# Long branch B: probabilities transposed in blocks of 32 by VectorE and through DRAM; value products by halves, three units behind

## The chip, the cores and the metric

The kernel runs on one NeuronCore of a Trainium2 chip. Its five engines have instruction streams of their own: TensorE (PE; PEld is its weight load), VectorE (DVE), ScalarE (ACT), GpSimd (POOL) and SyncE (SP). SP, ACT and POOL also issue DMA transfers, each from its own queue in order. The metric is the device time of one execution in microseconds; smaller is better.

## The reference

One layer of an encoder with two token mixers, on a prompt of 1024 tokens and a sample of 512, model width 1024, everything in float32. Branch A is grouped-query attention with rotary positions, branch B neighbourhood attention on a grid 64 tokens wide: a query sees a clamped window of 8 rows by 16 columns, with a learned bias. Cut to what matters here:

```python
def _token_mixer(xn, ...):
    z = xn @ w_in                       # q, k, v of both branches, two gates
    o_a = _gqa_attention(qa, ka, va)
    o_b = _neighbourhood_attention(qb, kb, vb, rpb)
    merged = sigmoid(ga) * (o_a @ w_proj_a) + sigmoid(gb) * (o_b @ w_proj_b)
    return merged @ w_out

    # _neighbourhood_attention, for each block of 128 queries
    s = einsum('bqhd,bkhd->bhqk', qi, kb) * scale + bias
    s = where(mask, s, NEG_INF)
    p = softmax(s, axis=-1)
    return einsum('bhqk,bkhd->bqhd', p, vb)
```

Two residual blocks (this mixer, then an MLP with squared ReLU) and a final norm follow.

## The kernel before

Products of full accuracy are made of three PE products in a reduced format: each operand is split into a high part (a ScalarE copy that rounds, `hi`) and the rest (`lo`, source minus `hi`, mostly on VectorE). The helper `mm3` (L195 to L197) adds hi x hi, hi x lo and lo x hi into one PSUM bank. `load_cols` (L223) brings weights by SP into one of three staging buffers (`raw_tile`, 3 buffers shared by all such loads of the long run) and splits them (`split`, L184 on ScalarE, L190 on VectorE).

`run` handles the sample first (512 tokens, `NB` = 1) and then the prompt (1024 tokens, `NB` = 2, "long"). In each, branch A comes first, then branch B, then both projections. The change is in branch B of the long run, the phase `phB`.

Branch B works in 32 units: 8 heads times 4 strips `j` of 16 query columns, in the order 1, 2, 0, 3. A unit of the long run has two halves (`hf`) of 128 queries (8 rows by 16 columns), and for each half 384 keys (12 rows by 32 columns).

- `s_unit`: two score products a half (L971) into the PSUM tile `sb` ("sbs" in the profile, two buffers of pool `pbig`), VectorE adds bias and mask, negates and reduces (L974), ScalarE takes the exponential and its sum (L979), VectorE the reciprocal (L981), POOL scales (L982) to the probabilities `pb` ("pbs"). POOL also adds bias and mask (`bms`, L957). `prep` brings a head's bias (`rects`) and value strips (`vss`, sixteen DMAs, L878).
- `t_unit`: PE transposes 128x128 blocks of `pb` by products with the identity (L994), three a half, into PSUM `ptb`; ScalarE rounds them into `bh` (L999), VectorE subtracts for the rest (L1000).
- `v_unit`: value strips times transposed probabilities (L1013) into `ob`: key blocks 1 and 2 for both halves (512 columns: hi and lo times 256 queries), blocks 0 and 3 for one half each (256 columns). `finish_o` adds the parts and sends heads 0 to 5 to DRAM (`obd`); heads 6 and 7 stay.

The loop calls `s_unit` for unit i, `t_unit` for unit i - `LS`, `v_unit` for unit i - `LS` - `LV` (both 1 in the long run). Between them, `fill.pull` takes PE work from generators: the branch B gate (`gate`, "gpss") and, for the last eight units, branch A's output projection (`proj_a`, "ppas": eight columns of weights `raw_pas`, activations `rawos` split into `oXs`, gate values `zas`). Every eight units `qkproj` makes queries and keys of the next two heads ("pqbs", "pkbs").

This order of calls is not the order on the engines. The tile scheduler orders each engine's stream when the program is built, and it moves loads and products ahead where their buffers are free in its plan. On the chip every stream, SP's DMA queue too, runs in that fixed order, and an instruction that waits holds all behind it.

## Time and profile before

| what | value |
|---|---|
| median of 3 runs | 2145.7 us (2145.51 to 2145.97) |
| profiled execution, first to last instruction (its span) | 2144.2 us |
| branch B of the long run in it | 777 to 1067 us |
| PE, granted clock | busy in 99% of the span, 0.999 of full speed |
| HBM | 264.85 MB read, 87.88 MB written |

The profiled execution has only its span on record; the runs lie about 1.5 us above it, from what stands before the first and after the last instruction. In rows of instruction groups the order is: line, engine, operation, out<-in, shapes, count, then busy us and mean ns, then idle time of the engine before them and who ended it. Rows of the timeline are: start, duration, engine, line, operation. A PE product's shown duration includes its way through the array; how long it holds PE is read from the distance of the starts.

### The profile page before, as it was taken

Reading aid. Unit: us, or ns where it says so; the run is one execution under the profiler, and the core shown is the slowest. Engines: PE = TensorE matmul, PEld = TensorE weight load, DVE = VectorE, ACT = ScalarE, POOL = GpSimd, SP = SyncE. Lnnn points to the kernel's source line nnn. Section 1 sums busy time; section 2 is a strip of 40 time slices with the busy share of each in tenths; the row PEclk is TensorE's granted clock in tenths of the full one; section 3 lists DMA queues with packets and bytes.
Section 4 is the critical chain, followed back from the end, with each engine's and each line's share of the span. In section 5 each row is a group of like instructions: output and inputs, shape, how many; then the busy total and the mean of one; then the engine's idle time right before and its main releaser. Section 6 shows DMA issues by size and latency. Waiting matters only on the chain.

```text
span 2144.2 us, 32083 instructions
## 1 busy us (share of the span) xinstructions
PE 2116.2 (99%) x10967; PEld 1847.3 (86%) x10967; DVE 1462.7 (68%) x2793; ACT 1146.2 (53%) x2511; POOL 356.1 (17%) x446
## 2 busy tenths in 40 slices
PE   9999999999999999999999999999999999999998
PEld 8888778888897888887888899999999988888886
DVE  6665786767657755656882877777777777659563
ACT  6664653767566644555530566566655643434342
POOL 2232310323232223333200200003000000000000
PEclk9999999999999999999999999999999999999999
DMA  6437557520122133444472665578545799688561
GB/s 190 133 98 212 152 162 251 186 71 25 57 79 68 42 95 108 131 118 112 140 240 103 213 194 184 171 248 205 165 142 157 256 353 343 212 279 281 165 206 59
DMA packets 321259, 354.08 MB, mean 165 GB/s; under 512 B 31551, under 2 KB 255431, under 8 KB 321095
## 3 DMA queue, kind: packets, MB, share of 16 engines
q1 hardware_dynamic: 277927, 279.65, 41.9%
q10 hardware_dynamic: 36016, 52.19, 7.0%
q0 software_dynamic: 7152, 20.19, 3.5%
q8 instruction: 87, 1.43, 0.3%
q14 instruction: 77, 0.63, 0.1%
HBM read 264.85 MB, written 87.88 MB: 165 GB/s over the span
## 4 chain that ended last, share of the span: by engine, by line
PE 67%; DVE 1%; issue 1%; DMA 0%; ACT 0%; POOL 0%; SPq 0%; POOLq 0%; ACTq 0%; DVEq 0%
PE dn L195 6%; PE dn L196 6%; PE dn L197 6%; PE ua L195 2%; PE ua L196 2%; PE ua L197 2%; PE ud L195 2%; PE ud L196 2%; PE ud L197 2%; PE uc L195 2%; PE uc L196 2%; PE uc L197 2%; PE gpss L195 2%; PE gpss L197 2%; PE gpss L196 2%; PE ops L197 1%
## 5 line engine op out<-in xcount | busy, mean ns | idle before, releaser
L197 PE MATMUL dn<-wd,al 128*128 128x512 f32 x624 | 242.8, 389 | 0.0
L196 PE MATMUL dn<-wd,ah 128*128 128x512 f32 x624 | 242.8, 389 | 0.0
L195 PE MATMUL dn<-wd,ah 128*128 128x512 f32 x624 | 242.7, 389 | 0.0
L1273 ACT ACTIVATE ah<-ar 128x512 fp32r<-128x512 f32 x168 | 104.4, 628 | 203.1 <-PE dn L196 177.1
L1274 DVE TENSOR_TENSOR al<-ar,ah 128x512 fp32r<-128x512 f32 x168 | 113.9, 685 | 71.6 <-ACT ah L1273 64.0
L197 PEld LDWEIGHTS dn<-wd,al 128*128 128x128 f32 x624 | 117.1, 188 | 24.4
L195 PEld LDWEIGHTS dn<-wd,ah 128*128 128x128 f32 x624 | 117.1, 188 | 24.3
L196 PEld LDWEIGHTS dn<-wd,ah 128*128 128x128 f32 x624 | 117.1, 188 | 24.2
L749 POOL TENSOR_SCALAR ps<-ps,rls 128x1024 f32<-128x1024 f32 (+1 forms) x96 | 96.8, 1010 | 225.7 <-DVE rls L748 200.4
L788 ACT ACTIVATE pths<-pTs 128x512 fp32r<-128x512 f32 x160 | 94.0, 597 | 74.0 <-PE pTs L783 71.9
L789 DVE TENSOR_TENSOR ptls<-pTs,pths 128x512 fp32r<-128x512 f32 x160 | 107.6, 686 | 37.7 <-ACT pths L788 36.9
L743 DVE TENSOR_REDUCE nms<-ss 128x1 f32<-128x1024 f32 (+1 forms) x96 | 99.8, 1040 | 25.6 <-PE ss L741 25.0
L195 PE MATMUL gpss<-xs_0h,w_gs 128*128 128x512 f32 x256 | 105.5, 412 | 0.5 <-DVE ot_Bs L440 0.4
L746 ACT ACTIVATE ps<-ss,nms 128x1024 f32<-128x1024 f32 (+1 forms) x96 | 93.2, 972 | 22.8 <-DVE nms L743 20.2
L783 PEld LDWEIGHTS pTs<-ident,ps 128*128 128x128 f32 x640 | 77.9, 140 | 28.5 <-POOL ps L749 4.3
L180 POOL TENSOR_TENSOR rs_f<-ms_f,mhalf 128x1 f32<-128x1 f32 x6 | 4.0, 667 | 590.7 <-DVE ms_f L176 590.7
L197 PE MATMUL gpss<-xs_0h,w_gs 128*128 128x512 f32 x256 | 101.1, 395 | 0.2 <-DVE w_gs L190 0.2
L196 PE MATMUL gpss<-xs_0l,w_gs 128*128 128x512 f32 x256 | 101.0, 394 | 0.0
L783 PE MATMUL pTs<-ident,ps 128*128 128x128 f32 x640 | 99.0, 274 | 1.3 <-DVE ptls L789 0.6
L1273 ACT ACTIVATE A<-S 128x512 fp32r<-128x512 f32 x128 | 75.9, 623 | 31.5 <-DVE S L1336 22.7
L957 POOL TENSOR_TENSOR bms<-rects,msks 128x384 f32<-128x384 f32 (+1 forms) x72 | 70.1, 977 | 129.1 <-DVE nmbs L974 107.6
L1392 ACT ACTIVATE c<-c 128x384 f32<-128x384 f32 x96 | 50.3, 524 | 69.4 <-DVE c L1391 69.3
(330 smaller groups left out, 6419.7 us busy)
## 6 DMA issues: line engine op xcount, KB each, us to landing
ar<-ud SPq DMA_DIRECT2D x120, 512.0 KB, 5.3
br<-in_w_mlp_down_dram SPq DMA_DIRECT2D x72, 512.0 KB, 5.2
rawu<-in_w_mlp_up_dram SPq DMA_DIRECT2D x64, 512.0 KB, 4.1
ud<-c ACTq DMA_DIRECT2D x128, 192.0 KB, 3.2
raw_gs<-in_w_in_dram SPq DMA_DIRECT2D x32, 512.0 KB, 4.0
zgs<-sgs ACTq DMA_DIRECT2D x48, 256.0 KB, 2.2
ud<-cs SPq DMA_DIRECT2D x64, 192.0 KB
raw_os<-in_w_out_dram SPq DMA_DIRECT2D x16, 512.0 KB, 3.9
```

Source lines behind the costliest of these rows:

```text
L195: nc.tensor.matmul(out, ah, bh, start=start, stop=False, **kw)
L196: nc.tensor.matmul(out, ah, bl, start=False, stop=False, **kw)
L197: nc.tensor.matmul(out, al, bh, start=False, stop=stop, **kw)
L743: nc.vector.tensor_reduce(nm_, s, axis=AX.X, op=ALU.max, negate=True)
L746: nc.scalar.activation(p, s, AF.Exp, bias=nm_, accum_out=l)
L749: nc.gpsimd.tensor_scalar(p, p, rl, 1.0, op0=ALU.mult, op1=ALU.mult)
L783: nc.tensor.transpose(pt[:, j * P : (j + 1) * P], PP[u, j][:, kc * P : (kc + 1) * P], ident)
L788: nc.scalar.activation(hi, pt, AF.Copy)
L789: nc.vector.tensor_tensor(lo, pt, hi.bitcast(F32), op=ALU.subtract)
L957: nc.gpsimd.tensor_tensor(bm.rearrange("p (r c) -> p r c", c=32), rects[h][:, ir : ir + kr_n, jr : jr + 32], msk[:, hf * 3 + ct, :].rearra ...
L1273: nc.scalar.activation(hi, src, AF.Copy)
L1274: nc.vector.tensor_tensor(lo, src, hi.bitcast(F32), op=ALU.subtract)
```

## The change

For the long run only (`moved`): the exponential writes its 384 columns into one tile `pb` for both halves, ordered by 32-column block. VectorE transposes the 128x768 tile in place in blocks of 32x32 (L1001 of the changed kernel). SP writes it to a DRAM tile (`tbs`, L1003), and one step later, in `fetch_t`, reads it back with four DMAs (L1012) so that the four 32-row groups of queries stand beside each other and keys lie on partitions. The four reads land in the lo part of `bh` (three buffers instead of two); `t_unit` is then one ScalarE copy of 768 columns for hi (L1022) and one POOL subtraction in place for lo (L1023). The PE transposes, their PSUM tiles, and the two copies and two VectorE subtractions are gone in the long run. `v_unit` makes six products of 256 columns, one for each half and key block (L1049), instead of four. `LS` is 2 for both runs, so value products come three units behind the scores. `pb` has two buffers of twice the size instead of four. `finish_o` takes `os` at the width it uses.

```diff
--- before.py
+++ after.py
@@ -443,12 +443,12 @@
                 nc.scalar.activation(t[:, :n], o[HD:P, :n], AF.Copy)
             if parts is not None:
                 hi, lo, ps = parts
-                b = pool.tile([P, 512], F32, tag="os", name=f"os_{nm}", bufs=2)[ps, :n]
+                b = pool.tile([P, n], F32, tag="os", name=f"os_{nm}", bufs=2)[ps, :n]
                 nc.vector.tensor_tensor(b, o[0:HD, :n], t[:, :n], op=ALU.add)
                 nc.scalar.activation(hi, b, AF.Copy)
                 nc.vector.tensor_tensor(lo, b, hi.bitcast(F32), op=ALU.subtract)
                 return
-            b = pool.tile([HD, 512], F32, tag="os", name=f"os_{nm}", bufs=2)
+            b = pool.tile([HD, n], F32, tag="os", name=f"os_{nm}", bufs=2)
             nc.vector.tensor_tensor(b[:, :n], o[0:HD, :n], t[:, :n], op=ALU.add)
             nc.scalar.dma_start(dst, b[:, :n])
 
@@ -861,6 +861,7 @@
             msk = ph.tile([P, halves * 3, nkey], BF16, tag="msk", name=f"msk{N}", bufs=1)
             nc.gpsimd.dma_start(msk, w["mask2"] if halves == 2 else w["mask1"])
             rects, strips, bms, PT = {}, {}, {}, {}
+            moved = NB == 2
 
             def raw_here(name):
                 if NB == 2:
@@ -948,6 +949,8 @@
                 jr = (16, 8, 8, 0)[j]
                 s = big(f"sb{N}_{h}_{j}")
                 ps = []
+                if moved:
+                    pm = ph.tile([P, 4, halves, nkc, 32], F32, tag="pb", name=f"pb{N}_{h}_{j}", bufs=2)
                 for hf in range(halves):
                     nm = f"{N}_{h}_{j}_{hf}"
                     r0 = 0 if hf == 0 else 4
@@ -974,18 +977,51 @@
                     nc.vector.tensor_tensor_reduce(
                         out=sb, in0=so, in1=bm, op0=ALU.add, op1=ALU.min, scale=-1.0, scalar=3e38, accum_out=nm_
                     )
-                    p = ph.tile([P, nkey], F32, tag="pb", name=f"pb{nm}", bufs=4)
                     l = sml.tile([P, 1], F32, tag="l", name=f"lb{nm}")
-                    nc.scalar.activation(p, sb, AF.Exp, bias=nm_, scale=-1.0, accum_out=l)
+                    if moved:
+                        p = pm[:, :, hf]
+                        nc.scalar.activation(
+                            p.rearrange("p b k i -> p k b i"),
+                            sb.rearrange("p (k b i) -> p k b i", b=4, i=32),
+                            AF.Exp,
+                            bias=nm_,
+                            scale=-1.0,
+                            accum_out=l,
+                        )
+                    else:
+                        p = ph.tile([P, nkey], F32, tag="pb", name=f"pb{nm}", bufs=4)
+                        nc.scalar.activation(p, sb, AF.Exp, bias=nm_, scale=-1.0, accum_out=l)
                     rl = sml.tile([P, 1], F32, tag="rl", name=f"rlb{nm}")
                     nc.vector.reciprocal(rl, l)
                     nc.gpsimd.tensor_scalar(p, p, rl, 1.0, op0=ALU.mult, op1=ALU.mult)
                     ps.append(p)
                 PT[u] = ps
+                if moved:
+                    blocks = pm.rearrange("p b f k i -> p (b f k) i")
+                    nc.vector.transpose(blocks, blocks)
+                    turned = dram.tile([P, 4, halves * nkc * 32], F32, name=f"tb{N}_{h}_{j}")
+                    nc.sync.dma_start(turned, pm.rearrange("p b f k i -> p b (f k i)"))
+                    PT[u] = turned
+
+            def fetch_t(u):
+
+                h, j = u
+                hl = ph.tile([P, 2, 4, halves, nkc, 32], F32R, tag="bh", name=f"bh{N}_{h}_{j}", bufs=3)
+                turned = PT[u].rearrange("(a i) b w -> b i a w", i=32)
+                for b in range(4):
+                    nc.sync.dma_start(
+                        hl[b * 32 : b * 32 + 32, 1].rearrange("p a f k i -> p a (f k i)").bitcast(F32), turned[b]
+                    )
+                PT[u] = hl
 
             def t_unit(u):
                 h, j = u
                 nm = f"{N}_{h}_{j}"
+                if moved:
+                    hi, lo = (PT[u][:, i].rearrange("p a f k i -> p (a f k i)") for i in range(2))
+                    nc.scalar.activation(hi, lo.bitcast(F32), AF.Copy)
+                    nc.gpsimd.tensor_tensor(lo, lo.bitcast(F32), hi.bitcast(F32), op=ALU.subtract)
+                    return
                 pt = [mm(f"ptb{nm}_{hf}") for hf in range(halves)]
 
                 hl = ph.tile([P, rows // 4, 2, halves, P], F32R, tag="bh", name=f"bh{nm}", bufs=2)
@@ -1005,10 +1041,19 @@
                 nm = f"{N}_{h}_{j}"
                 hl = PT.pop(u)
                 o = mm(f"ob{nm}")[:, : 2 * nq].rearrange("p (i q) -> p i q", i=2)
-                if halves == 2:
-                    seq = [(1, 0, 2), (2, 0, 2), (0, 0, 1), (3, 1, 2)]
-                else:
-                    seq = [(0, 0, 1), (1, 0, 1)]
+                seq = [(0, 0, 1), (1, 0, 1)]
+                if moved:
+                    seq = []
+                    for hf in range(halves):
+                        for k in range(nkc):
+                            nc.tensor.matmul(
+                                o[:, :, hf * P : (hf + 1) * P],
+                                strips[h][:, j, hf + k, :],
+                                hl[:, :, :, hf, k, :],
+                                start=(hf + k == 0),
+                                stop=(hf == halves - 1 and k == nkc - 1),
+                                skip_group_check=True,
+                            )
                 for n, (kc, a, b) in enumerate(seq):
                     nc.tensor.matmul(
                         o[:, :, a * P : b * P],
@@ -1035,7 +1080,7 @@
                 pass
             units = [(h, j) for h in range(8) for j in (1, 2, 0, 3)]
             n = len(units)
-            LS, LV = (1, 1) if NB == 2 else (2, 1)
+            LS, LV = 2, 1
             qp = None
             held = []
             for i in range(n + LS + LV):
@@ -1058,6 +1103,8 @@
                         qp = None
                         if i + 1 < n - 8:
                             wqk = load_qk(i // 8 + 2, held)
+                if moved and 0 <= i - 1 < n:
+                    fetch_t(units[i - 1])
                 fill.pull(f // 2)
                 if 0 <= i - LS < n:
                     t_unit(units[i - LS])
```

The scheduler's order changes with it. Names carry the long run's numbers: `sbs_6_1` are the scores of head 6, strip 1; the last number is a buffer's. First PE, where the last keys are made (`pkbs_3_1`) and branch A's output projection (`ppas`) begins. Before:

```order
L197 MATMUL pkbs_3_1_11531<-xs_1h_4943,w_bks_3_10823 128x512
L994 MATMUL ptbs_5_0_0_11563<-ident,pbs_5_0_0_11341 128x128 x3
L994 MATMUL ptbs_5_0_1_11564<-ident,pbs_5_0_1_11354 128x128 x3
L1013 MATMUL obs_5_2_11576<-bhs_5_2_11399,vss_5_10896 128x512 x2
L1013 MATMUL obs_5_2_11576<-bhs_5_2_11399,vss_5_10896 128x2x128 x2
L971 MATMUL sbs_6_1_11587<-kBs_3_0_11361,qBs_3_11360 128x384
L971 MATMUL sbs_6_2_11710<-kBs_3_0_11361,qBs_3_11360 128x384
L971 MATMUL sbs_6_1_11587<-kBs_3_0_11361,qBs_3_11360 128x384
L971 MATMUL sbs_6_2_11710<-kBs_3_0_11361,qBs_3_11360 128x384
L994 MATMUL ptbs_5_3_0_11633<-ident,pbs_5_3_0_11470 128x128 x3
L994 MATMUL ptbs_5_3_1_11634<-ident,pbs_5_3_1_11483 128x128 x3
L195 MATMUL ppas_0_0_11677<-oXs_0_0_11654,w_pas_0_11648 128x512
```

In the changed program the last keys are followed by the six value products of 5_1 and the first two score products of 6_1 and of 6_2 (not shown); from there, up to the first product of the projection:

```order
L974 MATMUL sbs_6_1_11526<-kBs_3_0_11306,qBs_3_11305 128x384 x2
L974 MATMUL sbs_6_0_11727<-kBs_3_0_11306,qBs_3_11305 128x384 x2
L974 MATMUL sbs_6_2_11647<-kBs_3_0_11306,qBs_3_11305 128x384 x2
L974 MATMUL sbs_6_3_11811<-kBs_3_0_11306,qBs_3_11305 128x384 x2
L974 MATMUL sbs_6_0_11727<-kBs_3_0_11306,qBs_3_11305 128x384 x2
L974 MATMUL sbs_7_1_11897<-kBs_3_1_11307,qBs_3_11305 128x384 x2
L974 MATMUL sbs_6_3_11811<-kBs_3_0_11306,qBs_3_11305 128x384 x2
L974 MATMUL sbs_7_2_11973<-kBs_3_1_11307,qBs_3_11305 128x384 x2
L195 MATMUL ppas_0_0_11612<-oXs_0_0_11589,w_pas_0_11583 128x512
```

The scores of six units now stand together ahead of the projection, where the scores of two and the transposes stood.

Second, SP's queue up to the projection's loads (`raw_pas`: weights, `rawos`: branch A's output). Before:

```order
L223 DMA raw_gs_3328_7_0_10981<-in_w_in_dram 128x8x128
L878 DMA vss_5_10896<-vds_4660 32x4x128 x16
L223 DMA raw_pas_0_0_11646<-in_w_proj_a_dram 128x4x128
L872 DMA rects_6_11203<-biases 128x768
L814 DMA rawos_0_0_11652<-oads_4663 128x1024
L878 DMA vss_6_11205<-vds_4660 32x4x128 x16
L814 DMA rawos_0_1_11655<-oads_4663 128x1024
```

And in the changed program:

```order
L1012 DMA bhs_5_0_11506<-tbs_5_0_11303 32x4x192 x4
L873 DMA rects_7_11555<-biases 128x768
L879 DMA vss_7_11557<-vds_4660 32x4x128 x7
L1003 DMA tbs_6_1_11553<-pbs_6_1_11527 128x768
L879 DMA vss_7_11557<-vds_4660 32x4x128 x9
L1012 DMA bhs_5_3_11574<-tbs_5_3_11430 32x4x192 x4
L223 DMA raw_pas_0_0_11581<-in_w_proj_a_dram 128x4x128
L814 DMA rawos_0_0_11587<-oads_4663 128x1024
L814 DMA rawos_0_1_11590<-oads_4663 128x1024
L814 DMA rawos_0_2_11593<-oads_4663 128x1024
L1003 DMA tbs_6_2_11670<-pbs_6_2_11648 128x768
```

The first weights stood behind the strip loads of head 5; now they stand behind the write of unit 6_1, the strip loads of head 7 and the fetch of 5_3.

Third, SP's queue in the changed program at head 3's strip loads and at the last units' weights:

```order
L1003 DMA tbs_2_1_10101<-pbs_2_1_10075 128x768
L879 DMA vss_3_10105<-vds_4660 32x4x128 x16
L1012 DMA bhs_1_3_10122<-tbs_1_3_9950 32x4x192 x4
L223 DMA raw_gs_3328_4_0_10141<-in_w_in_dram 128x8x128
L1003 DMA tbs_2_2_10190<-pbs_2_2_10168 128x768
```

```order
L1003 DMA tbs_7_2_11996<-pbs_7_2_11974 128x768
L1012 DMA bhs_7_1_11998<-tbs_7_1_11924 32x4x192 x4
L223 DMA raw_pas_5_0_12003<-in_w_proj_a_dram 128x4x128
L843 DMA zas_4_0_12011<-zgs_0_4661 128x512
L843 DMA zas_4_1_12030<-zgs_0_4661 128x512
```

Before, these loads had no write or fetch ahead of them: the gate weights `raw_gs_3328_4` stood ahead of head 3's strip loads.

## The prediction

> **What bounds the kernel now.** I read the page's shares first, then the stage that the diff touches by its windows (branch B of the long sequence, 777 to 1067 us), the chain of waits inside it, and the queue of SP.
>
> ```profile
> span 2144.2 us, 32083 instructions
> PE 2116.2 (99%) x10967; PEld 1847.3 (86%) x10967; DVE 1462.7 (68%) x2793; ACT 1146.2 (53%) x2511; POOL 356.1 (17%) x446
> 777.00:1067.00 290.00, 288.43 (x1399) 237.21 (x1398) 180.98 (x487) 150.23 (x315) 95.39 (x120) 1.00 0.43 124
> ```
>
> The columns of the last row are length, busy PE, PEld, DVE, ACT and POOL, granted clock, DMA share, GB/s. PE works in 288.43 of the stage's 290.00 us at full clock: whatever leaves PE shortens the stage, and whatever makes PE wait lengthens it, one for one. The chain shows what the edit touches, and two stretches of PE its pace:
>
> ```profile
> 1039.40 0.66 PE ptbs L994 x6
> 1042.81 0.69 PE obs L1013 x4
> 288.05 0.39 PE L196 MATMUL ppas<-oXs,w_pas 128*128 128x512 f32 x1
> 288.27 0.39 PE L197 MATMUL ppas<-oXs,w_pas 128*128 128x512 f32 x1
> 288.50 0.40 PE L1013 MATMUL obs<-bhs,vss 128*128 128x256 f32 x2
> 288.74 0.41 PE L971 MATMUL sbs<-kBs,qBs 128*128 128x256 f32 x2
> 288.98 0.39 PE L195 MATMUL ppas<-oXs,w_pas 128*128 128x512 f32 x1
> ```
>
> A unit's six transposes hold PE for 0.66 us, its four value products for 0.69. Starts 0.23 us apart give a 512-column product's pace, and 0.24 for two of 256 columns gives 0.12 each.
>
> **The change part by part.** PE loses 32 x 0.66 = 21.1 us. The value products become six of 256 columns, 6 x 0.12 = 0.72 instead of 0.69, so +1.0 us. **PE's work: -20.1 us.**
>
> What replaces the transposes runs on the other engines:
>
> ```profile
> L1000 DVE TENSOR_TENSOR bhs<-ptbs,bhs 128x384 fp32r<-128x384 f32 x64 | 33.0, 549 | 8.3 <-ACT bhs L999 7.9
> L190 DVE TENSOR_TENSOR oXs<-rawos,oXs 128x512 fp32r<-128x512 f32 x14 | 9.3, 691 | 0.4 <-ACT oXs L184 0.4
> L190 DVE TENSOR_TENSOR w_pas<-raw_pas,w_pas 128x256 fp32r<-128x256 f32 x16 | 6.0, 415 | 1.2 <-ACT w_pas L184 1.2
> L999 ACT ACTIVATE bhs<-ptbs 128x384 fp32r<-128x384 f32 x64 | 28.5, 488 | 8.3 <-PE ptbs L994 6.7 <-ACT pbs L979 0.8
> L184 ACT ACTIVATE w_pas<-raw_pas 128x512 fp32r<-128x512 f32 x8 | 5.0, 629 | 3.4 <-DMA raw_pas<-in_w_proj_a_dram 2.6 <-PE pkbs L196 0.7
> L184 ACT ACTIVATE oXs<-rawos 128x1024 fp32r<-128x1024 f32 x7 | 7.2, 1052 | 0.6 <-DMA rawos<-obds 0.6
> L957 POOL TENSOR_TENSOR bms<-rects,msks 128x384 f32<-128x384 f32 x48 | 51.4, 1072 | 93.4 <-DVE nmbs L974 83.7 <-DMA msks<-in_mask_dram 7.2 <-DVE rlbs L981 2.4
> L982 POOL TENSOR_SCALAR pbs<-pbs,rlbs 128x384 f32<-128x384 f32 x64 | 39.7, 625 | 44.7 <-DVE rlbs L981 24.0 <-PE ptbs L994 9.3 <-PE ppas L197 6.7
> ```
>
> VectorE drops 33.0 us and gains 32 block transposes of 128x768, an operation that the trace doesn't have. From 415 ns at 256 columns, 549 at 384 and 691 at 512 the line reaches 0.96 us at 768; bounds 0.55 (as long as 384) and 1.9 (twice the line); I take 0.95, the nearest operation's line: 30 us, 3 less than it drops. The Trainium skill ("Vector Engine (DVE) Microarchitecture Reference", "The reshape front-end and per-opcode configuration") has the block transpose take one element per cycle and lane; no run so far shows that. ScalarE drops 28.5 us and gains 32 copies of 768 columns, 0.83 us each (between 488 ns at 384 and 1052 at 1024): 27 us. POOL gains 32 subtractions of 768 columns: at least 2 x 625, at most 2 x 1072 ns; I take 1.9 us, near the two-operand row: 61 us, so 156 of 290. All three stay far below the stage's length. Their sums are covered by PE's work; their places in the queues are not.
>
> SP gains five issues a unit: one write that waits for VectorE, and four reads that wait for the write before. They go into the one queue that also brings weights and values.
>
> ```profile
> vss<-vds SPq DMA_DIRECT2D x112, 64.0 KB, 2.3
> raw_gs<-in_w_in_dram SPq DMA_DIRECT2D x5, 512.0 KB, 3.8
> raw_pas<-in_w_proj_a_dram SPq DMA_DIRECT2D x8, 256.0 KB, 4.1
> rawos<-obds SPq DMA_DIRECT2D x3, 512.0 KB, 3.6
> SPq L843 <- DVE mAs L850: 17.3, 9, 4.9
> 925.39 7.70 SPq L878 DMA_DIRECT2D vss<-vds  x16
> 937.09 0.39 SPq L223 DMA_DIRECT2D raw_pas<-in_w_proj_a_dram  x1
> 945.87 0.33 SPq L814 DMA_DIRECT2D rawos<-oads  x1
> ```
>
> The last numbers of the DMA rows are us from issue to landing. The wait row shows SP standing up to 4.9 us behind one buffer's release, with all behind it; sixteen strip loads take 7.70 us, so 0.48 us an issue. The first weights of branch A's output projection were issued at 937.09, 67 us before PE used them (below). In the changed order they stand behind the write of unit 6_1, nine strip loads and a fetch.
>
> The Trainium skill ("DMA: Bandwidth & Descriptors", "Anatomy of one DMA") states the same: a DMA's semaphore wait happens on the issuing sequencer before dispatch. By that rule a load behind an unready write is late by the whole wait; the trace's row above agrees.
>
> How long until a unit's write can go, and what PE had at the place in question:
>
> ```profile
> 883.44 0.52 PE L971 MATMUL sbs<-kBs,qBs 128*128 128x384 f32 x2
> 883.80 0.40 PE L195 MATMUL gpss<-xs_1h,w_gs 128*128 128x512 f32 x1
> 884.73 0.63 PE L971 MATMUL sbs<-kBs,qBs 128*128 128x384 f32 x2
> 887.16 1.14 POOL L982 TENSOR_SCALAR pbs<-pbs,rlbs 128x384 f32<-128x384 f32 x2
> 999.91 0.82 PE L994 MATMUL ptbs<-ident,pbs 128*128 128x128 f32 x6
> 1002.77 0.62 PE L971 MATMUL sbs<-kBs,qBs 128*128 128x384 f32 x2 [0.79 <-DVE kBs L937]
> 1004.55 0.50 PE L195 MATMUL ppas<-oXs,w_pas 128*128 128x512 f32 x1
> ```
>
> Two score products hold PE for 0.36 us (883.44 to 883.80). From the start of a unit's second pair (884.73) to the end of its scaling (888.30) are 3.6 us; with the transpose 4.5, with the issue 4.9.
>
> *Place 1, the start of the output projection.* T is the end of the key projection (999.91 before). The scores of 6_1 come at T+2.9 (1002.77), their second half at T+3.2; the write is ready at T+7.7, T+8.6 with the two more reductions that VectorE has ahead. Issue T+9.0; nine strip loads T+13.3; four fetches T+15.2; the weights land 4.1 later at T+19.3, ScalarE splits them by T+19.9 (629 ns) and the first activations by T+21.0 (1052 ns), where PE starts. PE's own work until then is one value product and ten score halves, 0.72 + 3.6 = 4.3, so it idles 16.7 us. Before, the same stretch was 4.64 us (999.91 to 1004.55) with 2.6 of work (twelve transposes, a value product, four score products). **+14.5 us.** The next activations wait for three staging buffers: the third set of activations is issued only when VectorE has split the weights (T+20.8), the fourth when it has split the first set (T+22.4; 2 x 691 ns); the fourth lands at T+26.0 and, behind two exponentials on ScalarE, is split at about T+29, while PE has 7.4 us of products from T+21.0: **+3 us** (0 to 5).
>
> *Places 2 and 3, the heads whose strip loads stand between a write and the next fetch.* After the scores of 2_1: write out at 4.7 us, sixteen loads 12.4, fetch 14.3, landed 16.6 (like the 64 KB rows), copied 17.4, subtracted 19.3. PE has 53 x 0.23 + 2 x 0.72 + 8 x 0.36 = 16.5 us: +2.8. After 4_1, with eleven loads: 16.9 against 15.4, +1.5, then gate weights that are ready at 19.5 where PE comes at 18.3, +1.2. **+5.5 us.**
>
> *Place 4, the last units.* The weights of column 5 stand behind the write of 7_2 and a fetch: 4.7 + 1.9 + 4.1 + 0.6 = 11.3 us after its scores, where PE has 7.6 (24 x 0.23, a value product, four score halves): +3.7; column 6 +1.0, the start of the next stage +1.0. **+5.7 us.**
>
> Elsewhere fetches are hidden: a value product comes some 25 us after its unit's scores, and the way there (4.9, then 2.3 each for write and read, 1.9 of issue, 0.8, 1.9) is 14.
>
> **Sum**: -20.1 + 14.5 + 3 + 5.5 + 5.7 = +8.6 us on a span of 2144.2; the runs' median of 2145.7 is 1.5 above the span, so **2154 us**.
>
> **The rivals.** *The loads come in time* (the other side): if SP ran ahead and PE waited only at places 2 and 3, 2145.7 - 20.1 + 5.5 = 2131. For it: PE waits 1.6 us in the whole stage now. Against: the weights stand behind a write that needs scores which PE computes just before. It decides if PE starts the output projection within 5 us of T. *Place 1 alone costs*: 2145.7 - 20.1 + 17.5 = 2143; places 2 to 4 are margins of 1 to 4 us, and shorter landings would close them. *Transfers get in each other's way*: 32 x 2 x 0.39 MB = 25 MB come on top of the stage's 36 (124 GB/s x 290 us), so a DMA share of 0.43 x 61/36 = 0.73; were landings to double, place 1 gains 4 + 4, places 2 and 3 two each, place 4 six: +18, 2172. For it: strip-sized packets; against: a share still below 1. That the transposes stay on PE is excluded: the changed order has none in this stage.
>
> **How the numbers follow.** Forecast 0.52 (its own range 2147 to 2162), in time 0.18, place 1 alone 0.16, crowded transfers 0.14. Place 1 with every duration at its lower bound (transpose 0.55, landings 2.3) is still +11, with the other places at zero 2137; doubled landings give 2172. Range 2137 to 2171. About 0.2% (4.3 us) is what a measurement here can tell from no change. Faster takes 0.18 and a quarter of "place 1 alone": 0.22; same the rest of it and a tenth of the forecast: 0.17; slower 0.61.
>
> **What would show it.** The six transposes gone from the chain, value products of about 0.72 us a unit, and DVE below 200 us in the stage. The first ppas product about 21 us after the last pkbs one, with SP standing at L1003 just before; a wait of some us at the value product of 1_3; ppas of column 5 released by raw_pas. The stage near 299 us. I am wrong if the stage is below 285, or if PE's idle time sits elsewhere, above all on bhs.

## The result, and the profile after

| | us |
|---|---|
| before, median of 4 runs | 2145.84 (2145.51 to 2146.36) |
| changed, median of 4 runs | 2224.84 (2222.26 to 2225.98) |
| ratio, with its 95% interval | 1.0368 (1.0354 to 1.0381) |

The change costs 79.0 us, where +8.6 was forecast: the direction was right, the size nine times too small, and the time lies 54 us above the range. The page of the changed kernel begins:

```profile
span 2222.3 us, 32032 instructions
PE 2128.6 (96%) x10839; PEld 1849.0 (83%) x10839; DVE 1480.4 (67%) x2761; ACT 1143.0 (51%) x2479; POOL 408.1 (18%) x478
```

PE is busy 12 us more than before, though 20 us of work were taken from it, and idle besides. Everything happens in branch B. Before, the stage is 777 to 1067, and 1077.2 us follow it to the end of the span. Counted back from the end by the same 1077.2 us, the changed kernel's stage is 777 to 1145. Its windows, with the columns as in the prediction (length, busy PE, PEld, DVE, ACT, POOL, granted clock, DMA share, GB/s):

```profile
777.00:800.00 23.00, 23.00 (x102) 18.54 (x101) 10.46 (x28) 8.21 (x13) 4.17 (x5) 1.00 0.50 138
800.00:1038.00 238.00, 201.93 (x873) 163.26 (x873) 117.80 (x292) 96.68 (x192) 107.06 (x112) 0.91 0.54 161
1038.00:1061.00 23.00, 9.26 (x27) 5.09 (x26) 13.73 (x33) 9.65 (x20) 12.96 (x15) 0.61 0.43 131
1061.00:1145.00 84.00, 66.80 (x276) 51.73 (x277) 55.54 (x104) 32.72 (x61) 23.09 (x20) 0.87 0.57 178
sum 368.00, PE 301.00 PEld 238.61 DVE 197.53 ACT 147.27 POOL 147.28; mean PE 75.25 PEld 59.65 DVE 49.38 ACT 36.82 POOL 36.82
```

Two things fill the 78 us. **Idle time**: 368.0 - 301.0 = 67.0 us, against 1.6 before; 36 of it before the output projection, 14 at its start, 17 behind. **Slow products**: the work was 288.4 - 20.1 = 268.3 us, and PE took 301.0 for it, 32.7 more. The column of the granted clock, 1.00 before, says why: 0.91, 0.61, 0.87. In the trace's record of the clock it is 0.50 for stretches in which PE is busy for 54 us of the stage; at full speed that work takes half, so some 27 us are lost. The other 5 or so may be the ends of products ahead of a wait, which nothing covers. PE's timeline shows how that looks:

```profile
889.69 0.98 PE L974 MATMUL sbs<-kBs,qBs 128*128 128x384 f32 x4
894.20 1.65 PE L1049 MATMUL obs<-bhs,vss 128*128 128x256 f32 x6 [3.53 <-POOL bhs L1023]
895.65 0.63 PE L195 MATMUL gpss<-xs_0h,w_gs 128*128 128x512 f32 x1
896.07 0.63 PE L196 MATMUL gpss<-xs_0l,w_gs 128*128 128x512 f32 x1
...
899.81 0.40 PE L196 MATMUL gpss<-xs_0l,w_gs 128*128 128x512 f32 x1
900.04 0.39 PE L197 MATMUL gpss<-xs_0h,w_gs 128*128 128x512 f32 x1
```

PE waits 3.5 us for a unit's split probabilities. The value products behind take twice their time (1.45 us from start to next start, for six of 0.12), and so do the gate products: starts 0.42 us apart, and 0.23 again from 899.81. This wait of 3.5 us costs some 2.5 more in slow products (half of the 5.4 from 894.20 to the clock's return at 899.66).

The engines' new work is what the prediction took it for (columns: line, engine, shapes, count, then busy and mean ns, then idle before):

```profile
L1023 POOL TENSOR_TENSOR bhs<-bhs 128x768 fp32r<-128x768 f32 x32 | 59.1, 1846 | 82.9 <-ACT bhs L1022 60.1 <-DMA bhs<-tbs 9.6 <-PE ppas L197 8.4
L1001 DVE STREAM_TRANSPOSE pbs<-pbs 128x768 f32<-128x768 f32 x32 | 31.1, 973 | 25.3 <-POOL pbs L996 23.5 <-DMA bhs<-tbs 1.6
L1022 ACT ACTIVATE bhs<-bhs 128x768 fp32r<-128x768 f32 x32 | 26.9, 841 | 26.8 <-DMA bhs<-tbs 9.5 <-DVE os_Bs L452 5.8 <-DVE nmbs L977 3.6
```

973, 841 and 1846 ns stand against 950, 830 and 1900. What was not foreseen is when they come. One unit, strip 3 of head 0, through four queues:

```profile
810.80 0.52 PE L974 MATMUL sbs<-kBs,qBs 128*128 128x384 f32 x2
```

```profile
818.46 0.34 SPq L1003 DMA_DIRECT2D tbs<-pbs  x1
818.90 1.91 SPq L1012 DMA_DIRECT2D bhs<-tbs  x4
822.51 0.34 SPq L1003 DMA_DIRECT2D tbs<-pbs  x1
822.90 12.70 SPq L879 DMA_DIRECT2D vss<-vds  x14
839.98 1.73 SPq L1012 DMA_DIRECT2D bhs<-tbs  x4
```

```profile
849.01 0.60 ACT L429 ACTIVATE sgs<-gpss 128x512 f32<-128x512 f32 x1 [12.95 <-PE gpss L197]
849.64 0.33 ACTq L430 DMA_DIRECT2D zgs<-sgs  x1
850.15 0.84 ACT L1022 ACTIVATE bhs<-bhs 128x768 fp32r<-128x768 f32 x1 [0.54 <-DMA raw_gs<-in_w_in_dram]
```

The scores start at 810.80 and the write goes out at 818.46; with 2.7 us from issue to landing (the row of `tbs` in the DMA issues) it is in DRAM at 821.2. Its reads go out at 839.98: in SP's order they stand behind the reads of the unit before, the write of the unit after, and fourteen strip loads. With 2.4 us to landing they are there by 843.7. The copy runs at 850.15, since ScalarE stood 12.95 us for a gate product and then issued that result's transfer. The wait that the profile names in the copy's own row is the last 0.54 us only; the rest is in the row two lines above it. POOL subtracts until 853.0, where PE, which came to the value products after 849, starts them: 42 us after the scores, for a way that the prediction summed to 14.

Over all 32 units, from the trace: 45.8 us from scores to the end of lo in the median. On the mean the write goes out 4.0 us after the transpose, the first read 14.4 after the write (2.7 of it landing), and the copy starts 9.0 after the last read was issued (2.4 of it landing).

### The profile page after: what moved, and what is told of

The parts are those of the page before. It is cut to its first block, busy times and chain, and to the rows that moved or that the text cites. A ratio compares the mean times of both kernels' runs of the same rounds, so it can differ in the third digit from the quotient of the medians.

```text
span 2222.3 us, 32032 instructions
## 1 busy us (share of the span) xinstructions
PE 2128.6 (96%) x10839; PEld 1849.0 (83%) x10839; DVE 1480.4 (67%) x2761; ACT 1143.0 (51%) x2479; POOL 408.1 (18%) x478
## 4 chain that ended last, share of the span: by engine, by line
PE 53%; DVE 3%; DMA 3%; issue 2%; POOL 2%; ACT 1%; SPq 0%; POOLq 0%; ACTq 0%; DVEq 0%
PE dn L196 6%; PE dn L197 6%; PE dn L195 6%; PE ud L195 2%; PE ud L196 2%; PE ua L196 2%; PE ua L197 2%; PE ud L197 2%; PE ua L195 2%; PE uc L196 2%; PE uc L197 2%; PE uc L195 2%; PE ops L196 1%; PE ops L195 1%; PE ops L197 1%
## 5 line engine op out<-in xcount | busy, mean ns | idle before, releaser
L1321 DVE TENSOR_TENSOR A<-S,A 128x512 fp32r<-128x512 f32 x128 | 84.5, 686 | 4.1 <-ACT A L1320 4.1
L195 PE MATMUL ud<-B,A 128*128 128x384 f32 x256 | 85.7, 335 | 0.7 <-DVE c L1438 0.7
```

Source lines behind the costliest of these rows:

```text
L195: nc.tensor.matmul(out, ah, bh, start=start, stop=False, **kw)
L1321: nc.vector.tensor_tensor(lo, src, hi.bitcast(F32), op=ALU.subtract)
```

## The experiments

All are edits of the changed kernel unless it is said otherwise. Times are medians, differences against the changed kernel's 2224.84; the kernel before ran beside each at 2145.2 to 2145.8. "The sum" is the time without waits: 2145.8 - 20.1 = 2125.7 for the changed kernel.

**First round: is it SP's completion marks, SP's queue, the length of the way, the clock?** The operand fields of the trace name a semaphore for each transfer's completion. Eight of them go round among the transfers of SP and ScalarE, and an issue waits until the one before on its mark has landed. In the changed kernel's waits of SP's queue 23 stops in the stage, 86 us in all, end with a ScalarE transfer of results or gate values (the expectation has a narrower count, 19 and 69), and many of these transfers stood for PE; this looked like a closed loop.

```diff
-                    nc.scalar.dma_start(dst[c * P : (c + 1) * P, tb * 512 : tb * 512 + 512], sg)
+                    (nc.gpsimd if NB == 2 and goff == 3328 else nc.scalar).dma_start(...)
-            nc.scalar.dma_start(dst, b[:, :n])
+            (nc.gpsimd if NB == 2 and nm[0] == "B" else nc.scalar).dma_start(dst, b[:, :n])
```

> The changed kernel, with ScalarE's 40 transfers of the stage (gate values to DRAM, value results to DRAM) issued by POOL, whose transfers have completion marks of their own. Theory 'shared marks': SP's issue stands for one of eight completion marks that it shares with ScalarE's transfers, and those stand for PE's products; 19 stops of SP (69 us in the stage) end 1.9 to 3.5 us after the issue of the ScalarE transfer that held the mark. Without them PE's waits for bhs between 800 and 1030 us (some 36 us, and half-clock time behind them) mostly go: 2170 to 2195 us. Rival 'writes at the head of the queue': SP stands for VectorE's transposes and the strip loads alone, nothing changes: 2215 to 2235. POOL can get in its own way (it stands for the gate values): that would also show as 2215 or more, but with bhs late behind POOL's issues.

2224.81 us, no change. The stops went: in this kernel the fourteen strip loads take half the time.

```profile
823.97 7.00 SPq L879 DMA_DIRECT2D vss<-vds  x14
831.07 1.89 SPq L1012 DMA_DIRECT2D bhs<-tbs  x4
```

7.00 us instead of 12.70, and the reads 9 us earlier than in the changed kernel, for nothing. ScalarE came to this unit's copy when it did before (850.15), since it stood for the gate product as long:

```profile
849.53 0.60 ACT L429 ACTIVATE sgs<-gpss 128x512 f32<-128x512 f32 x1 [13.03 <-PE gpss L197]
850.03 0.83 ACT L1022 ACTIVATE bhs<-bhs 128x768 fp32r<-128x768 f32 x1
```

SP itself now stood 140 us at its writes instead of 88. The theory of the marks falls.

```diff
-                    nc.sync.dma_start(turned, ...)
+                    nc.gpsimd.dma_start(turned, ...)
-                    nc.sync.dma_start(hl[b * 32 ...], turned[b])
+                    nc.gpsimd.dma_start(hl[b * 32 ...], turned[b])
```

> The changed kernel, with the write and the four reads of each unit issued by POOL. SP's queue is then as before the change. Theory 'the queue of SP' in both forms (marks, writes at its head): the first product of the output projection comes within 6 us of the last key product again and the waits for weights go; POOL gains 160 issues of about 0.6 us (the row of kBs), 96 us. 2150 to 2190. Rival 'the way is too long': a unit's way from scores to value products takes longer than three units in any queue, and POOL's issues lengthen it: 2220 or more.

2198.98 us, -25.9: a third of the loss, less than expected. As expected, the projection's first product follows the last key product closely again (1021.62 behind 1020.67), without a wait of its own. But PE now waits 6.9, 6.6 and 6.7 us at the value products of 4_2, 7_0 and 7_3.

```diff
-            LS, LV = 2, 1
+            LS, LV = (3 if NB == 2 else 2), 1
-                if moved and 0 <= i - 1 < n:
-                    fetch_t(units[i - 1])
+                if moved and 0 <= i - 2 < n:
+                    fetch_t(units[i - 2])
```

> The changed kernel with the reads two units behind the scores and the value products four behind (LS 3, fetch at i - 2), three buffers of bh as they are. Theory 'the way is too long': one unit more (8.4 us) covers most of the waits for bhs between 800 and 1030 us: 2165 to 2190, with the starts of both projections as late as they are. Theory 'shared marks': SP's stops are as many and as long, and only their part below 8.4 us is covered: 2185 to 2210. Writes at the head of SP's queue stay: place 1 still near 20 us.

2216.95 us, -7.9. More distance in the program helps little, below both forecasts.

```diff
+                    for _ in range(12):
+                        nc.tensor.matmul(o[:, 0, :], strips[h][:, j, 0, :], strips[h][:, j, 0:2, :], start=True, stop=True, skip_group_check=True)
                     for hf in range(halves):
```

> The changed kernel with twelve more PE products of 256 columns ahead of each unit's value products, into the same PSUM tile, which the value products then overwrite: 32 x 12 x 0.12 = 46 us of PE work. Theory 'the clock': PE's products ran at half clock behind its longer waits and cost some 33 us; filled waits keep the clock up. Of the 46 us some 36 fall into waits, and 15 to 20 us of slow products go: 2212 to 2235, granted clock near 0.99. Rival 'the clock falls for another reason': clock near 0.98 as it is, 2235 to 2250. If the filler does not fall into the waits: 2260 to 2271.

2218.21 us: 46 us of useless work make the kernel 6.6 us *faster*. The stage's window (to 1077.2 us before the end, as in all that follow):

```profile
777.00:1137.70 360.70, 327.86 (x1655) 273.49 (x1654) 188.30 (x451) 146.97 (x282) 147.67 (x152) 0.95 0.56 165
```

Idle 32.8 us instead of 67.0, and 327.9 - 268.3 - 46.1 = 13.5 us beyond the work instead of 32.7; the clock is 0.95, over the changed kernel's stage 0.89. That waits slow the clock is shown; the cost is 19 us by this difference, 27 by the clock record above.

**Second round: is it the turn from one unit to the next?** ScalarE's order has a unit's copy behind the previous unit's results, and these behind its value products.

```diff
-                    nc.gpsimd.tensor_tensor(lo, lo.bitcast(F32), hi.bitcast(F32), op=ALU.subtract)
+                    nc.vector.tensor_tensor(lo, lo.bitcast(F32), hi.bitcast(F32), op=ALU.subtract)
```

> The changed kernel with the subtraction for lo on VectorE instead of POOL. Theory 'the turn': ScalarE's order has the copy hi of a unit behind the previous unit's results (L439, and the transfer L453 that stands for VectorE's add), though the fetched data have lain there for 5 to 13 us; so a turn from one unit's value products to the next's takes 1.0 + 0.6 + 1.9 + 0.6 + 0.85 + 1.85 = 6.9 us, more than PE has in its order at some places. The subtraction should take about 1.0 us instead of 1.82, so some 0.8 us less a turn: 2195 to 2215 us. Rival 'transfers late' (SP's queue holds the reads): no change, 2218 to 2232.

2203.81 us, -21.0, as the turn forecast.

```diff
-                    nc.scalar.activation(hi, lo.bitcast(F32), AF.Copy)
-                    nc.gpsimd.tensor_tensor(lo, lo.bitcast(F32), hi.bitcast(F32), op=ALU.subtract)
+                    nc.gpsimd.tensor_copy(hi, lo.bitcast(F32))
+                    nc.vector.tensor_tensor(lo, lo.bitcast(F32), hi.bitcast(F32), op=ALU.subtract)
```

> The changed kernel with hi copied by POOL (about 1.2 us, twice the 0.58 of its scaling) and lo subtracted by VectorE (about 1.0). Theory 'the turn': ScalarE and its transfers are out of it, a turn is 1.0 + 0.6 + 1.1 + 1.0 = 3.7 us, shorter than PE's work between value products; the waits for bhs between 800 and 1030 us go, those at the starts of both projections stay: 2170 to 2195. Rival 'transfers late': 2215 to 2232.

2200.49 us, -24.4: between the two forecasts, a miss for both. With ScalarE out of the turn it is only 3 us better than the edit before.

```diff
-            (ScalarE's two transfers of e1 by nc.scalar)
+            (the same by nc.sync)
```

> The changed kernel with the stage's results and gate values (ScalarE's 40 transfers) issued by SP. Theory 'the turn': hi stands no longer behind the wait for VectorE's add and the issue, a turn of about 4.5 us: 2180 to 2205. Rival 'the queue of SP': SP now stands for each unit's results itself, and the reads come later still: 2230 or more.

2211.23 us, -13.6, between the two.

```diff
-                if i == n - (12 if first else 8):
+                if i == n - 12:
```

> The changed kernel, with the output projection's first weights and activations asked for four steps earlier (at i == n - 12), so that they stand ahead of the write of unit 5_2 and not behind that of 6_1. Place 1 of the prediction (PE waits 18 us around the first product of the projection, at half clock): it goes to under 6 us, 2198 to 2212. Rival: PE's order has six units' scores ahead of the projection anyway, and their reductions set the pace: 2216 to 2226.

2216.58 us, -8.3, at the rival's edge. The projection's first product, 6.0 us late in the changed kernel, now comes without a wait (1041.14), but its second column of weights is 3.0 us late. And where PE waited 6.0 us for the probabilities of 4_3, behind the scores of 5_3, it now waits 9.6: the key products need a weight split that stands on ScalarE behind the projection's activations, whose load SP issued late. The loads crowd there instead.

**Third round: what is left without PE's wait, and do the cures add up?** First the kernel before with nothing changed but the value products:

```diff
-                    seq = [(1, 0, 2), (2, 0, 2), (0, 0, 1), (3, 1, 2)]
+                    seq = [(hf + k, hf, hf + 1) for hf in range(2) for k in range(nkc)]
```

> The kernel before, with its value products alone changed to six of 256 columns (PE's transposes, distances and queues as before). The prediction's term: +0.03 us a unit, +1.0 us in all: 2146 to 2148 us. Rival: the smaller products cost more than their columns, or change the scheduler's order: 2150 or more.

2146.18 against 2145.84, ratio 1.0003 (0.9995 to 1.0012): +0.3 us (-1.1 to +2.6), and the +1.0 of the prediction lies within.

```diff
+                if one:
+                    BH0.append(hl)
...
                 hl = PT.pop(u)
+                if moved:
+                    hl = BH0[0]
```

> The changed kernel, with every unit's value products reading the split probabilities of the first unit, in a buffer of its own (the others' are still transposed, written, read back and split into two buffers, but nobody reads them): the output is wrong in branch B for that. PE then never waits for the round trip. Theory 'the turn': the waits for bhs go, all along the stage and at its end, with the half-clock time behind them; place 1 stays (some 18 us, and slow products): 2145.7 - 20 + 18 + 10, so 2145 to 2170. Rival 'the rest of the engines are slowed by the queues and transfers as such': 2195 or more.

This kernel leaves out the use of the trips: all value products read the first unit's probabilities, so PE waits for no other trip. 2203.94 us, -20.9: of the 79 us, 58 are left, as the rival forecast. The turn, as the main cause, falls too. Its windows, ahead of the projection, at its start and behind:

```profile
777.00:1013.60 236.60, 214.75 (x976) 174.61 (x974) 127.86 (x319) 104.82 (x204) 109.69 (x116) 0.96 0.57 170
1013.60:1039.56 25.96, 8.47 (x22) 4.54 (x20) 12.41 (x33) 9.84 (x21) 14.73 (x16) 0.59 0.57 164
1039.56:1123.60 84.04, 66.32 (x276) 51.77 (x277) 54.09 (x105) 32.93 (x61) 22.88 (x20) 0.87 0.60 178
```

PE is idle 22, 17 and 18 us there, against 36, 14 and 17 in the changed kernel. So 31 of the changed kernel's 67 us of idle time do not hang on PE's wait for a trip: they lie at the projection's start and behind it. Ahead of the projection PE now waits for VectorE's reductions, which wait for ScalarE and POOL, which stand in their own order for copies whose reads are late. (The other units share two buffers here instead of three, which may delay their reads; this was not separated.)

> Three single edits together: the trip's write and reads by POOL, lo on VectorE, results and gate values by SP. Alone they gave -26, -21 and -14 us against the changed kernel. If they cure different waits they add up: 2160 to 2172; if they cure the same waits: 2178 to 2200. Faster than the kernel before only if all idle time goes, which neither theory expects.

2169.30 us, -55.5: nearly the sum of the three single gains (25.9 + 21.0 + 13.6 = 60.5). So they cure mostly different waits.

> As the three edits together, and the reads two units behind the scores, the value products four (alone -8 us). Adding up: 2150 to 2165; overlapping: 2170 to 2195.

2165.32 us, -59.5, at the edge of adding up, still 0.87% (0.72 to 1.03) above the kernel before and 40 above its sum.

**Fourth round: does each trip cost, or their crowding?** In these, strips 1 and 0 (every second unit) go the new way, in e15 and e16 of heads 0 to 5 alone. The others keep PE's transposes, with six value products and one unit less distance. The scheduler's order changes with it at the output projection: its first product stands behind six score products (four in the kernel before, twenty in the changed one), and its first weights are loaded early. In e17 (below), which has the same order as e14 and e16, SP issues them ahead of the write of 4_1, 67 us before their use:

```profile
930.71 0.40 SPq L223 DMA_DIRECT2D raw_pas<-in_w_proj_a_dram  x1
936.75 0.34 SPq L1009 DMA_DIRECT2D tbs<-pbs  x1
```

```diff
+            def mv(u):
+                return moved and (u[1] in (1, 0))
-                if moved:
+                if mv(u):
...
+                for d in (2, 1) if moved else (LS,):
+                    if 0 <= i - d < n and (not moved or d == (2 if mv(units[i - d]) else 1)):
+                        t_unit(units[i - d])
```

> Strips 1 and 0 of every head go the new way (16 units), strips 2 and 3 by PE's transposes (value products one unit earlier); trip by POOL, lo on VectorE, results by SP as in the run of the three edits. PE's work: -16 x 0.66 + 1 = -9.6 us, so 2136 without any wait. That run lay 44 us above its own sum (2169.3 against 2145.8 - 20.1). 'Each trip has its own wait': half of it, 2158 (2152 to 2164). 'Crowding': a quarter or less, 2138 to 2147.

2157.29 us, ratio 1.0056 (1.0044 to 1.0069): 21 us above its sum, half of the other's 44.

> The same 16 units, with the changed kernel's own queues (trip by SP, lo by POOL, results by ScalarE). The changed kernel lay 99 us above its sum. 'Each trip has its own wait': half, 2186 (2176 to 2196). 'Crowding': a quarter or less, 2140 to 2162.

2141.81 us, ratio 0.9982 (0.9973 to 0.9991). Half the trips, with the queues as the change has them, cost 6 us above their sum instead of 50, and the kernel is faster than the one before. That is what crowding forecast, but part of it is the other order at the projection: the 31 us of idle time there fall to 3 with it, and no run has one without the other. The three moved edits, cures at 32 trips, cost 15 us at 16; why stays open.

> As e13, but heads 6 and 7 wholly by PE's transposes: 12 units go the new way, none beside the output projection. PE's work -12 x 0.66 + 1 = -6.9: 2139 without any wait. 'Each trip has its own wait': 12/32 of 44, 2155. 'Crowding', with the projection's loads as the worst place: 2139 to 2146, and if below 2141 faster than both kernels.

2151.25 us, ratio 1.0026 (1.0017 to 1.0035): 12 us above its sum, between the two forecasts and nearer to that of each trip's own wait. With these edits the loss goes roughly with the number of trips (44, 21 and 12 us for 32, 16 and 12).

> The same 12 units with the trip by SP and results by ScalarE as in the changed kernel, lo on VectorE. That edit alone left 78 us above the sum (2203.8 against 2125.7). 'Each trip has its own wait': 12/32 of it, 2168. 'Crowding': 2140 to 2154.

2139.32 us, ratio 0.9970 (0.9959 to 0.9982): its sum of 2139 within a microsecond.

> 16 units (strips 1 and 0 of all heads), lo on VectorE, all else as in the changed kernel. Sum without waits 2145.8 - 9.6 = 2136. If the projection's start and end are the crowded places even with half the units: 2140 to 2150. If half the units leave room everywhere: 2135 to 2139.

2136.15 us, ratio 0.9958 (0.9945 to 0.9972), again within a microsecond of its sum: the fastest kernel of the study, 9 us faster than the one before and 89 faster than the changed one. Its stage:

```profile
777.00:1057.90 280.90, 278.49 (x1370) 232.46 (x1369) 194.27 (x484) 147.26 (x298) 96.21 (x120) 1.00 0.59 169
```

288.4 - 9.6 = 278.8 us of work forecast, 278.5 measured, 2.4 idle, clock 1.00.

```diff
-                return moved and (u[1] in (1, 0))
+                return moved and (u[0] < 6 and u[1] != 3)
```

> 18 units (strips 1, 2 and 0 of heads 0 to 5), lo on VectorE. Sum without waits 2145.8 - 18 x 0.66 + 1 = 2134.9. If what counts is whether neighbouring units take the trip (a trip's own time of about 22 us from scores to value products against 8.4 us a unit): 2145 to 2165. If it is the number of trips in the stage: 2134 to 2140.

2159.04 us, ratio 1.0066 (1.0053 to 1.0078), 24 us above its sum: 18 trips instead of 16, in neighbouring units, and it is 14 us slower than the kernel before. Its stage, the start of the projection in it, and SP's queue ahead of that:

```profile
777.00:1079.20 302.20, 285.64 (x1350) 233.44 (x1349) 196.51 (x487) 148.46 (x297) 93.99 (x120) 0.96 0.57 166
996.00:1030.00 34.00, 24.70 (x95) 17.51 (x94) 21.60 (x51) 17.11 (x32) 9.10 (x12) 0.70 0.50 152
989.65 17.58 SPq L882 DMA_DIRECT2D vss<-vds  x16
1007.28 0.43 SPq L223 DMA_DIRECT2D raw_pas<-in_w_proj_a_dram  x1
```

PE is idle 16.6 us in the stage, 9.3 of it at the projection's start, with 20 us at half clock. There the scheduler gathers the scores of five units again, and SP's weights stand behind strip loads; with every second unit it does neither. So some two thirds of the loss come from this order, though the units beside it (heads 6 and 7) take no trip, and PE's longest wait at a value product is 0.8 us. The time fits the forecast for neighbouring units; that they are its cause is not shown.

What differs between these kernels is seen in the units' ways, from the traces (us; means but for the median; the last two steps contain the landing of the write and of the reads, with medians of 2.3 to 4.2 us where the traces record it):

| kernel | trips | scores to lo, median | transpose to write | write to first read | last read to copy | above the sum |
|---|---|---|---|---|---|---|
| changed | 32 | 45.8 | 4.0 | 14.4 | 9.0 | 99 |
| e10, no wait for the trip | 32 | 42.5 | 4.1 | 13.4 | 7.7 | 78 |
| e12, three moved, lag 4 | 32 | 34.3 | 0.5 | 10.5 | 4.7 | 40 |
| e18, three of four | 18 | 29.9 | 2.3 | 6.8 | 9.0 | 24 |
| e17, every second | 16 | 20.5 | 0.0 | 3.2 | 7.3 | 0 |

SP's queue in e17 shows the reason for the fifth column:

```profile
811.88 0.34 SPq L1009 DMA_DIRECT2D tbs<-pbs  x1
812.27 1.92 SPq L882 DMA_DIRECT2D vss<-vds  x3
814.88 1.73 SPq L1018 DMA_DIRECT2D bhs<-tbs  x4
816.66 2.28 SPq L882 DMA_DIRECT2D vss<-vds  x4
825.79 0.34 SPq L1009 DMA_DIRECT2D tbs<-pbs  x1
826.17 3.05 SPq L882 DMA_DIRECT2D vss<-vds  x6
829.32 2.10 SPq L1018 DMA_DIRECT2D bhs<-tbs  x4
```

A unit's reads follow its own write and go out 3.0 us behind it (811.88 to 814.88), about when it has landed. With all units they stand behind the *next* unit's write, and this waits for scores that PE computes a unit later. That this order is the main part of the crowding ahead of the projection is argued from these rows and the table; a kernel with all units whose reads follow their own write was not run, so it is not shown.

## Why the prediction was right or wrong

- **PE's work, -20.1 us: right.** +0.3 (-1.1 to +2.6) for the split value products, and two kernels (e16, e17) that reach their sums within one.
- **Durations of the new work: right** (973, 841, 1846 ns against 950, 830, 1900). The block transpose's 973 ns for 768 elements a lane lie beside the 995 ns that VectorE took for a subtraction of the same shape in e5: it transposes at the pace of an operation element by element. The one element per cycle and lane that the prediction took from the Trainium skill ("Vector Engine (DVE) Microarchitecture Reference", "The reshape front-end and per-opcode configuration") fits this, though no run here isolates the cycle. Right, too, was "far below the stage's length" (DVE 197.5, POOL 147.3 of 368), but it decided nothing.
- **Place 1: right in mechanism and nearly in size, but for the clock.** PE's and SP's rows there:

```profile
1037.60 0.39 PE L197 MATMUL pkbs<-xs_1h,w_bks 128*128 128x512 f32 x1
1037.83 0.89 PE L1049 MATMUL obs<-bhs,vss 128*128 128x256 f32 x6
...
1060.97 0.79 PE L195 MATMUL ppas<-oXs,w_pas 128*128 128x512 f32 x1 [6.03 <-ACT oXs L184]
```

```profile
1030.25 4.00 SPq L879 DMA_DIRECT2D vss<-vds  x7
1048.24 0.34 SPq L1003 DMA_DIRECT2D tbs<-pbs  x1
1048.62 4.33 SPq L879 DMA_DIRECT2D vss<-vds  x9
1053.05 1.80 SPq L1012 DMA_DIRECT2D bhs<-tbs  x4
1054.89 0.43 SPq L223 DMA_DIRECT2D raw_pas<-in_w_proj_a_dram  x1
```

  The projection starts at T+23.1 (21.0 forecast), with the write at T+10.4 (9.0) and the weights at T+17.1 (15.2). SP stood 14 us at the write (1034.25 to 1048.24), with all of them behind it. The ten score halves came one by one, each behind VectorE's reductions, and at half clock from 1043 on (0.61 in the window 1038 to 1061).
- **Places 2 and 3: right as places, too small and too few.** PE waits 3.5 us at the value product of 1_3 (2.8 forecast), and 3.2 at that of 3_3 with 1.8 for gate weights behind it (1.5 and 1.2 forecast). But strip 3 of heads 0, 2 and 4 waits as well: 3.5, 4.0 and 6.0 us. **Place 4: too small**, 17.2 us idle from 1061 on, where 5.7 and the 3 for the later activations were forecast.
- **The step that failed** is "Elsewhere fetches are hidden: a value product comes some 25 us after its unit's scores, and the way there (...) is 14". It added durations and left out the waits between the queues, though the prediction had the rows for them: SP's order, quoted ahead of it, has the reads of 1_3 behind the write of 2_1. The way took 45.8 us in the median. Outside the named places PE stood some 27 us ahead of the projection (36 less the 8.5 of places 2 and 3), 21 of them at value products whose probabilities were not there.
- **A term that was missing**: what a wait does to PE's clock, some 27 us, nearly as much as all the idle time forecast (16.7 + 3 + 5.5 + 5.7). The sentence "whatever makes PE wait lengthens it, one for one" left it out. In the kernel before, whose longest wait in the stage was 0.79 us, nothing showed it. The Trainium skill ("TensorE: Matmul & The Clock Gate", "Part 1: The HAM clock gate (the "warmup" mystery)") has the array at half clock after an idle window of about 3.4 us, and back after a busy one. The length of the stretches agrees: nine at 0.50 begin in the stage, of 3.41, 6.83, 10.24 and 27.31 us, all multiples of 3.41, 85.3 us together. Their start does not: six times of nine the clock fell 1.7 to 2.7 us after PE's last product had ended, twice just behind a wait of over 3 us, and once 0.5 us after a short product among others. As an estimate from the page's window, each such wait would have had a second price of 1.7 us or more.
- **The rivals.** Transfers that get in each other's way: the trip's landings did not double (2.4 and 2.7 us against the 2.3 assumed, though the trace records only 14 of 128 reads and 4 of 32 writes), and the DMA share stayed at 0.54, below the 0.73 worked out. The two faster ones: excluded by the windows. The sign "PE's idle time sits elsewhere, above all on bhs" was named as what would make the forecast wrong, and it came: the largest part of PE's waits, 29.6 us in twelve, ends with POOL's subtraction.

## What to carry to other kernels

When PE is busy 99% of a stage, work taken from it and sent through four other in-order streams must be priced by the order of every queue that it enters: for each hop, what stands ahead and when *that* is ready. A sum of durations gives the shortest way, not the way. Do less of it than fits, and see what the scheduler makes of it elsewhere: sixteen trips, with another order at the next stage's loads, brought all that their sum promised, thirty-two lost 79 us. And add to each wait of PE over some 2 us the half-clock time behind it (in the changed kernel waits of up to 1.4 us ahead of the projection left the clock full, one of 2.3 did not).

## What was not expected of the hardware

- The clock fell to one half about 2.2 us into a wait (PE's last product ended at 914.48, the clock record has 0.50 from 916.72). The longest stretch at half clock, 27.3 us (1043.02 to 1070.32), spans pairs of short products with waits of 0.5 to 2.5 us between, a wait of 6.0, and 9 us of work behind it with one wait of 1.0.
- Useless products in front of a wait shortened the kernel by 6.6 us.
- SP's issues stop for completion marks that ScalarE's transfers hold, 86 us in the stage, and taking these stops away changed nothing: SP stood at its writes instead, and copies whose reads came earlier waited on ScalarE.
- Useful to know of the engines: POOL copied 128x768 values with rounding as fast as ScalarE (0.84 us each in e6 and the changed kernel), but took 1.85 us for the subtraction that VectorE did in 1.00 (e5).
